# Block 1 of a two-block model: modulation by groups of two chunks, the middle's elementwise work off GpSimd, filling products ahead of the inversion

## The chip, the cores and the metric

One core of one Trainium2 chip runs the whole kernel in one launch. TensorE (PE) multiplies, VectorE (DVE), ScalarE (ACT) and GpSimd (POOL) work elementwise, SyncE (SP) starts most transfers. The metric is the device time of an execution in microseconds (us).

## The reference, cut to what matters

512 tokens of 1024 features pass block 1 and then block 2 (attention, an MLP, a gated recurrence, an MLP). Only block 1 is changed:

```python
mod = jax.nn.silu(c) @ w_ada + b_ada                 # 1024 x 3072 weights, one row c
shift, scale, gate = jnp.split(mod, 3, axis=-1)
p = (x * (1 + scale) + shift) @ w_in                 # 512 x 1024 by 1024 x 3712
# branch A: u = gelu(p_u); v = layer_norm per head(gelu(p_v)) * ln_v_g + ln_v_b;
#           v = causal w_spatial over 128 tokens, per head, + b_spatial; u * v * silu(gate)
# branch B: p + mu * (previous token - p); then a recurrence over the tokens with
#           r, decay w, k, v, a, b for 8 heads of 64; layer norm per head; * silu(gate)
x = layer_norm(ALPHA * x + gate * (concat(A, B) @ w_out))
```

## The kernel before, in words

**Products.** Every operand of a large product is split into a high part (`wh`, `aH`) and the rest (`wl`, `aL`), both of a type that PE takes at full rate, and a product is three matmuls with 512 columns (`mm3`). A weight tile is loaded as `raw`, copied to `wh` by ACT (`copy`, L140) and subtracted to `wl` by DVE or GpSimd (`wsplit`, through `tt`, L123). There are three `raw` buffers and three weight slots.

**Start.** For each of the 8 chunks of 128 features, `load(k)` fetches 512 KB in each of two transfers of `w_ada` (`ada`, its columns for shift and scale), the chunk of `x` (`xt`) and 128 rows of `w_in`; rows of `w_ada` and `x` are 512 bytes long there. `ada_acc` multiplies and adds eight slices on DVE into two accumulators of 128x256 and adds these; two one-column matmuls sum over the partitions; `modulated(k)` turns `x`, applies scale and shift on ACT (`h32`), and makes `hH` (ACT) and `hL` (DVE). The chunk's 18 matmuls into six PSUM tiles follow (four for v of branch A, one each for the decay's and the first k columns). An order token fixes the instruction order of this stage on each engine. Behind it one GpSimd transfer of 2 MB stores ALPHA times x (`xaD`).

**Middle.** The list `ORDER` sets the order of 15 kinds of steps: `r`, `k` (products for branch B with the token shift, `shift_evac`), `A`, `n`, `t`, `m` (loads, layer norm, turns and mixing of branch A), `g` (the elementwise work of a pair of heads for the recurrence), `l` (`lmat`: 64x512 masks out of PSUM into the triangular matrices LB and LK), and `f` (filling products from a queue: V, the gate and u of branch A). `shift_evac` copies a PSUM tile to `sh` (ACT), subtracts neighbours into `shd` (GpSimd) and mixes (DVE, `stt`, L133). PSUM has two buffers `mm` and two `mg`, three `sm` and one `po` in this stage.

**Inversion.** The 32x32 triangular blocks go through DRAM (`scL`) into `XT`, and `inverse()` runs 31 steps of two dependent DVE instructions each (`bz`, then `TV`). On PE `fill(NFILL)` runs filling products meanwhile, three matmuls a step, out of the queue of `ugate` (u and gate of branch A, each a product, a split of weights on GpSimd, and `gt` or `mx` work).

**Chain.** Eight chunks of 64 tokens follow, each merged (`merge`, tiles `Tst`, `M`), with filling products of the four `gate(i)` between them, and `out_gate(k)` sums the third part of `mod` on DVE. Block 2, from about 430 us on, is not touched.

Tiles and order between the tokens come from the framework's scheduler, which fixes each engine's instruction order when the program is built.

## Time and profile before

| | |
|---|---|
| three runs | 1617.93, 1616.04, 1616.99 us (median 1616.99) |
| profiled execution, its own time | 1615.6 us |
| its span in the trace | 1613.8 us |
| PE busy in the span | 1542.8 us, 8293 matmuls |
| DVE, ACT, POOL busy | 939.0, 713.3, 329.5 us |

The stages of block 1 in the trace are the start (0 to 67.3 us, where the first product of the middle begins), the middle (to 179.7, the end of the last triangular mask), a stretch of transfers (to 192.5), the inversion (to 230.3) and the chain (from 239.1, its first merge). In what follows T0 is the first product of the middle. PE is busy for 96% of the span, so it idles for 71 us in all.

### The profile page before, as it was taken

To read this page: it belongs to the slowest core of one execution; us is meant where nothing else is said; L and a number is where in the kernel's file an instruction comes from. 1 tells how busy PE (TensorE), PEld (TensorE's weight loads), DVE (VectorE), ACT (ScalarE), POOL (GpSimd) and SP (SyncE) were. 2 spreads that over 40 slices of the span, in tenths; PEclk is the share of its full clock that TensorE was granted. 3 is DMA by queue.
4 is the path that set the end of the run, shared out by engine and by line. 5 is a ranking of instruction groups with operands and counts; after the bars stand their busy time and mean duration, and the time that the engine had idled before them with its cause. 6 is when DMAs were issued, how large, how long until landed. Compare 5 with 4: busy or idle time off the path is not lost. (4 is left out here: it accounts for less than half of the span.)

```text
span 1613.8 us, 21901 instructions
## 1 busy us (share of the span) xinstructions
PE 1542.8 (96%) x8293; PEld 1305.5 (81%) x8293; DVE 939.0 (58%) x1644; ACT 713.3 (44%) x1297; POOL 329.5 (20%) x459
## 2 busy tenths in 40 slices
PE   5987979999999999999999999999999999999998
PEld 4766768889978899888888887888888988888886
DVE  7797595678667739334343447667754824333445
ACT  3533314655565646333232335667745624322232
POOL 4464732224310023000000033223323200000000
PEclk9998989999999999999999999999999999999999
DMA  9732445544123132333333322322213223231421
GB/s 289 215 97 86 78 130 144 178 132 119 51 70 94 29 105 80 104 103 93 91 93 104 92 91 67 104 79 66 66 53 110 87 79 118 74 110 66 123 86 53
DMA packets 272893, 161.69 MB, mean 100 GB/s; under 512 B 29465, under 2 KB 253316, under 8 KB 272788
## 3 DMA queue, kind: packets, MB, share of 16 engines
q1 hardware_dynamic: 271492, 157.33, 34.2%
q0 software_dynamic: 1152, 2.70, 0.5%
q8 instruction: 65, 1.06, 0.3%
q14 instruction: 40, 0.33, 0.1%
q10 hardware_dynamic: 144, 0.26, 0.0%
HBM read 147.42 MB, written 11.53 MB: 98 GB/s over the span
## 5 line engine op out<-in xcount | busy, mean ns | idle before, releaser
L140 ACT CAST wh<-raw 128x1024 fp32r<-128x1024 f32 (+3 forms) x244 | 242.8, 996 | 466.0 <-PE mm L143 371.2
L123 DVE TENSOR_TENSOR wl<-raw,wh 128x1024 fp32r<-128x1024 f32 (+2 forms) x228 | 272.6, 1197 | 288.1 <-ACT wh L140 284.0
L143 PE MATMUL mm<-bL,wh 128*128 128x512 f32 (+1 forms) x752 | 282.2, 378 | 1.0 <-DVE bL L133 1.0
L143 PE MATMUL mm<-bH,wl 128*128 128x512 f32 (+1 forms) x752 | 281.7, 377 | 0.0
L143 PE MATMUL mm<-bH,wh 128*128 128x512 f32 (+1 forms) x752 | 279.4, 379 | 0.1
L143 PE MATMUL mm<-aH,wh 128*128 128x512 f32 (+1 forms) x656 | 241.0, 369 | 12.3 <-DVE gt L133 9.5
L143 PE MATMUL mm<-aH,wl 128*128 128x512 f32 (+1 forms) x656 | 236.8, 362 | 1.4 <-DVE wl L123 1.4
L143 PE MATMUL mm<-aL,wh 128*128 128x512 f32 (+1 forms) x656 | 237.7, 364 | 0.0
L143 PEld LDWEIGHTS mm<-bL,wh 128*128 128x128 f32 x752 | 141.1, 188 | 29.4 <-DVE bL L133 1.8
L143 PEld LDWEIGHTS mm<-bH,wl 128*128 128x128 f32 x752 | 141.1, 188 | 27.7
L143 PEld LDWEIGHTS mm<-bH,wh 128*128 128x128 f32 x752 | 139.2, 188 | 28.0 <-ACT hg_vt L137 0.5
L143 PEld LDWEIGHTS mm<-aH,wh 128*128 128x128 f32 x656 | 125.2, 191 | 34.4 <-DVE gt L133 10.5
L143 PEld LDWEIGHTS mm<-aH,wl 128*128 128x128 f32 x656 | 125.2, 191 | 20.7 <-DVE wl L123 1.9
L143 PEld LDWEIGHTS mm<-aL,wh 128*128 128x128 f32 x656 | 125.7, 192 | 18.3 <-issue 0.7
L143 PE MATMUL mm<-wh,aH 128*128 128x512 f32 x288 | 113.5, 396 | 1.5 <-ACT aH L140 1.5
L143 PE MATMUL mm<-wh,aL 128*128 128x512 f32 x288 | 112.8, 393 | 0.0
L143 PE MATMUL mm<-wl,aH 128*128 128x512 f32 x288 | 112.6, 393 | 0.0
L140 ACT CAST aH<-t 128x512 fp32r<-128x512 f32 (+1 forms) x74 | 41.1, 564 | 75.7 <-DVE t L123 75.5
L123 POOL TENSOR_TENSOR mlpt<-mlpt,sq 128x256 f32<-128x256 f32 (+1 forms) x9 | 11.9, 1320 | 306.6 <-ACT sq L137 306.6
L245 POOL TENSOR_TENSOR mlpss<-mlpss,pwm 128x1 f32<-128x1 f32 x4 | 2.2, 547 | 322.0 <-DVE mlpss L128 322.0
L123 DVE TENSOR_TENSOR aL<-t,aH 128x512 fp32r<-128x512 f32 (+1 forms) x74 | 45.1, 617 | 36.2 <-ACT aH L140 36.2
L143 PEld LDWEIGHTS mm<-wh,aH 128*128 128x128 f32 x288 | 54.6, 190 | 12.7 <-ACT aH L140 1.9
(545 smaller groups left out, 2819.7 us busy)
## 6 DMA issues: line engine op xcount, KB each, us to landing
raw<-in_mlp_w_dram SPq DMA_DIRECT2D x128, 512.0 KB
raw<-in_hgrn_w_in_dram SPq DMA_DIRECT2D x32, 512.0 KB
raw<-in_w_in_dram SPq DMA_DIRECT2D x23, 512.0 KB
ada<-in_w_ada_dram SPq DMA_DIRECT2D x16, 512.0 KB
raw<-in_w_out_dram SPq DMA_DIRECT2D x10, 512.0 KB
raw<-in_w_ada_dram SPq DMA_DIRECT2D x8, 512.0 KB
raw<-in_mla_w_o_dram SPq DMA_DIRECT2D x8, 512.0 KB
raw<-in_hgrn_w_o_dram SPq DMA_DIRECT2D x8, 512.0 KB
```

The lines of the kernel that those rows point to most:

```text
L123: self.st((eng or self.nc.vector).tensor_tensor(out=out, in0=a, in1=b, op=op))
L140: self.st(self.nc.scalar.copy(out=out, in_=in_))
L143: i = self.nc.tensor.matmul(out, l, r, start=start, stop=stop, **kw)
L245: self.nc.gpsimd.tensor_tensor(out=out, in0=a, in1=cst[: a.shape[0], :n], op=ALU.pow)
```

## The change

Start: loads and modulation go by groups of two chunks. A group is one 512 KB transfer of `x` and four 512 KB transfers of `w_ada`, with rows of 1 KB; one accumulator of 128x512 takes one `ts` and seven `stt`, the first four of them as soon as half of the group is there. The weight split of this stage is on DVE. A chunk's matmuls stand so that those with `hL` come last, and its `x` is turned ahead of the sums. `xaD` is stored by eight SP transfers between loads. The loads of `bsp` and `wsp` (branch A, 0.75 MB) stand among those of the start.

Middle: `shift_evac` is an ACT copy scaled by mu and one `stt` that reads PSUM; the subtraction and the memsets on GpSimd are gone. The row copy of `PC`, the affine `kf` and the broadcast copy `rx` go to ACT; two products and the LK mask go from GpSimd to DVE. The gain of branch A's layer norm is applied in the `stt` that mixes, and its bias comes in over eight small matmuls and four `stt` of 128x128.

Inversion: the first `gate` joins the queue, `NFILL` goes from 61 to 69 steps, and the splits and products of `ugate` go from GpSimd to DVE, at a priority that puts 7 splits, 3 `mx` and 4 `gt` between the steps of the inversion. Chain: `out_gate` uses one accumulator; eight filling steps fewer are left.

```diff
-NFILL = 61
+NFILL = 69
...
-        def ada_acc(acc, raw, steps=range(9)):
+        def ada_acc(acc, raw, steps, q0=0):
 
             for q in steps:
-                if q < 2:
-                    self.ts(acc[q], raw[:, q], sc[:, q : q + 1])
-                elif q < 8:
-                    self.stt(acc[q % 2], raw[:, q], sc[:, q : q + 1], acc[q % 2], ALU.mult, ALU.add)
+                if q == 0:
+                    self.ts(acc, raw[:, q - q0], sc[:, q : q + 1])
                 else:
-                    self.tt(acc[0], acc[0], acc[1], ALU.add)
+                    self.stt(acc, raw[:, q - q0], sc[:, q : q + 1], acc, ALU.mult, ALU.add)
...
-        xa = self.tl(sp, [P, 8, T], "xa", bufs=1)
-
-        def load(k):
+        xa = [self.tl(self.rp, [P, T], f"res{k}") for k in range(8)]
+
+        def load(g):
+
+            xt = self.tl(sp, [P, NB, 2 * P], "xt", bufs=2)
+            gs = slice(2 * g * P, (2 * g + 2) * P)
+            nc.sync.dma_start(out=xt, in_=xv[:, :, gs])
+            ada = []
+            for q in range(2):
+                raw = self.tl(sp, [P, 4, 2, 2 * P], "ada", bufs=4)
+                for j in range(2):
+                    src = w_ada[512 * q : 512 * q + 512, j * D + 2 * g * P : j * D + (2 * g + 2) * P]
+                    nc.sync.dma_start(out=raw[:, :, j, :], in_=src.rearrange("(k p) m -> p k m", p=P))
+                ada.append(raw)
+            return xt, ada, self.tl(sp, [P, 2, 2 * P], "acc")
...
         with self.ordered():
             self.petoken = "start"
-            ada_acc(cur[3], cur[1])
-            w_ = self.wsplit(cur[2], 1, 6 * P, nc.gpsimd)
-            h32 = modulated(0, cur[0], cur[3])
+            pt = turned_x(0, cur[0])
+            part(0, cur, 0)
+            part(0, cur, 1)
+            sums(0, cur)
+            w_ = self.wsplit(rv, 1, 6 * P)
+            modulated(0, pt)
             for k in range(8):
...
                 for tb in range(NB):
-                    s = slice(tb * P, (tb + 1) * P)
-                    self.mm3(psv[tb], hH[k][:, s], hL[k][:, s], wh[:, 0, :T], wl[:, 0, :T], k == 0, k == 7)
+                    self.mm(psv[tb], hH[k][:, tok[tb]], wh[:, 0, :T], k == 0, False)
+                    self.mm(psv[tb], hH[k][:, tok[tb]], wl[:, 0, :T], False, False)
                     if tb == SB and k < 7:
-                        w_ = self.wsplit(cur[2], 1, 6 * P, nc.gpsimd)
-                        h32 = modulated(k + 1, cur[0], cur[3])
...
+                        pt = turned_x(k + 1, (nxt if k % 2 else cur)[0])
+                        if k % 2:
+                            part(g + 1, nxt, 1)
+                            sums(g + 1, nxt)
+                            cur = nxt
+                        w_ = self.wsplit(rv, 1, 6 * P)
+                        modulated(k + 1, pt)
+                        if k % 2 == 0 and k < 6:
+                            part(g + 1, nxt, 0)
...
+                for tb in range(NB):
+                    self.mm(psv[tb], hL[k][:, tok[tb]], wh[:, 0, :T], False, k == 7)
+                for o, pz in oz:
+                    self.mm(pz, wh[:, 0, o : o + P], hL[k], False, k == 7)
             self.petoken = None
-            self.st(nc.gpsimd.dma_start(out=xaD.rearrange("k p t -> p k t"), in_=xa))
+            for k in range(8):
+                nc.sync.dma_start(out=xaD[k], in_=xa[k])
...
-            sh = self.tl(bp, [P, T + 1], "sh", bufs=2)
-            nc.gpsimd.memset(sh[:, 0:1], 0.0)
-            self.copy(sh[:, 1 : T + 1], ps)
-            d = self.tl(bp, [P, T], "shd", bufs=2)
-            self.tt(d, sh[:, 0:T], sh[:, 1 : T + 1], ALU.subtract, nc.gpsimd)
+            sh = shs[0]
+            shs.append(shs.pop(0))
+            self.act(sh[:, 1 : T + 1], ps, AF.Copy, scale=self.pc("mu_b", mc))
             o3 = lambda a: a.rearrange("p (c t) -> p c t", t=RC) if v3 else a
-            self.stt(out, o3(d), self.pc("mu_b", mc), o3(sh[:, 1 : T + 1]), ALU.mult, ALU.add)
+            self.stt(out, o3(ps), omu[:, mc : mc + 1], o3(sh[:, 0:T]), ALU.mult, ALU.add)
...
-            nc.gpsimd.tensor_copy(out=PCt[p], in_=eP[:, :, RC])
+            self.copy(PCt[p], eP[:, :, RC])
...
-            self.ts(kf, t2, hp[:, 8 + p : 9 + p], hp[:, 12 + p : 13 + p])
+            self.act(kf, t2, AF.Identity, scale=hp[:, 8 + p : 9 + p], bias=hp[:, 12 + p : 13 + p])
...
-            self.tt(AR[p][:, :, 1, :], AR[p][:, :, 1, :], eP[:, :, 1 : RC + 1], ALU.mult, nc.gpsimd)
+            self.tt(AR[p][:, :, 1, :], AR[p][:, :, 1, :], eP[:, :, 1 : RC + 1], ALU.mult)
...
-            self.tt(LK[p][hf], LK[p][hf], at(mk2).unsqueeze(1).to_broadcast([P, 4, P]), ALU.mult, nc.gpsimd)
+            self.tt(LK[p][hf], LK[p][hf], at(mk2).unsqueeze(1).to_broadcast([P, 4, P]), ALU.mult)
...
-            v2 = vg.rearrange("p h i -> p (h i)")
-            self.tt(v2, v2, lng, ALU.mult, nc.gpsimd)
-            self.tt(v2, v2, lnb, ALU.add)
-            return v2
+            return vg.rearrange("p h i -> p (h i)")
...
-                    evac(ps)
+                    with tc.high_priority(self.wprio):
+                        evac(ps)
...
-                self.tt(mx, mx, ug, ALU.mult, nc.gpsimd)
+                self.tt(mx, mx, ug, ALU.mult)
...
-                self.stt(t, t, 1.0, ps, ALU.add, ALU.mult)
+                x = self.tl(pool, [P, T], "gbn", bufs=1)
+                self.copy(x, ps)
+                self.stt(t, t, 1.0, x, ALU.add, ALU.mult)
...
-            yield from part_gemm(w_in, j * P, u_evac, nc.gpsimd)
-            yield from part_gemm(w_in, 1024 + j * P, g_evac, nc.gpsimd)
+            yield from part_gemm(w_in, j * P, u_evac)
+            yield from part_gemm(w_in, 1024 + j * P, g_evac)
...
+        queue.append(gate(0, rp))
+        self.wprio = 3000
         fill(NFILL)
+        self.wprio = 400
```

On DVE, in the start, from the accumulation for the second chunk to its modulation, before (`ada` is a slice of `w_ada`, `mod` the modulation):

```order
L128 TENSOR_SCALAR acc_45_208<-ada_200,sc 128x256
L128 TENSOR_SCALAR acc_46_209<-ada_200,sc 128x256
L133 SCALAR_TENSOR_TENSOR acc_45_208<-ada_200,sc,acc_45_208 128x256
L133 SCALAR_TENSOR_TENSOR acc_46_209<-ada_200,sc,acc_46_209 128x256
L133 SCALAR_TENSOR_TENSOR acc_45_208<-ada_200,sc,acc_45_208 128x256
L133 SCALAR_TENSOR_TENSOR acc_46_209<-ada_200,sc,acc_46_209 128x256
L133 SCALAR_TENSOR_TENSOR acc_45_208<-ada_200,sc,acc_45_208 128x256
L123 TENSOR_TENSOR aL_130<-h_41_195,aH_122 128x512
L133 SCALAR_TENSOR_TENSOR acc_46_209<-ada_200,sc,acc_46_209 128x256
L123 TENSOR_TENSOR acc_45_208<-acc_45_208,acc_46_209 128x256
L123 TENSOR_TENSOR mod<-sm_232,bada_111 128x2
```

and now, from the first chunk's split to that of the third:

```order
L122 TENSOR_TENSOR wl_202<-raw_178,wh_201 128x768
L122 TENSOR_TENSOR aL_130<-h_48_205,aH_122 128x512
L122 TENSOR_TENSOR wl_236<-raw_210,wh_235 128x768
L122 TENSOR_TENSOR aL_131<-h_57_239,aH_123 128x512
L127 TENSOR_SCALAR acc_222<-ada_216,sc 128x512
L132 SCALAR_TENSOR_TENSOR acc_222<-ada_216,sc,acc_222 128x512 x3
L132 SCALAR_TENSOR_TENSOR acc_222<-ada_219,sc,acc_222 128x512 x4
L122 TENSOR_TENSOR mod<-sm_282,bada_111 128x2x2
L122 TENSOR_TENSOR wl_289<-raw_262,wh_288 128x768
```

The 128x256 accumulation of every chunk with its closing addition has become one 128x512 accumulation for two chunks, and two weight splits have come in.

On DVE, in the middle, around the first `k` that is not of the start (`vn`, `lw` are branch A's norm, `ld`, `cum`, `kf`, `bz`, `BK` a pair of heads), before:

```order
L123 TENSOR_TENSOR vn_683<-vn_683,lnb 128x512
L590 TENSOR_REDUCE lw_940<-vn_689 128x8
L499 SCALAR_TENSOR_TENSOR cum_804<-m_676,ld_801 128x512
L123 TENSOR_TENSOR kf_814<-kf_814,k_116_661 128x512
L133 SCALAR_TENSOR_TENSOR k_129_759<-shd_794,pb,sh_791 128x512
L123 TENSOR_TENSOR vn_687<-vn_687,lw_928 128x512
L128 TENSOR_SCALAR lw_940<-lw_940 128x8
L123 TENSOR_TENSOR vn_685<-vn_685,lnb 128x512
```

and now:

```order
L122 TENSOR_TENSOR wl_792<-raw_789,wh_791 128x1024
L132 SCALAR_TENSOR_TENSOR AR_93<-po_662,omu,sh_593 128x8x64
L122 TENSOR_TENSOR vn_639<-vn_639,lw_864 128x512
L122 TENSOR_TENSOR wl_877<-raw_874,wh_876 128x1024
L132 SCALAR_TENSOR_TENSOR k_110_701<-mm_708,omu,sh_591 128x512
L129 TENSOR_SCALAR ld_739<-ld_739 128x512
L532 SCALAR_TENSOR_TENSOR cum_742<-m_624,ld_739 128x512
L122 TENSOR_TENSOR kf_752<-kf_752,k_101_613 128x512
```

The mixing `stt` reads the PSUM tile `mm` (or `po`) itself, the bias additions `lnb` have gone, and it stands sooner behind its product.

On DVE, in the inversion's eleventh to thirteenth steps, before:

```order
L123 TENSOR_TENSOR bz_1583<-XT_1581,TV_1582 128x220
L123 TENSOR_TENSOR TV_1582<-TV_1582,bz_1583 128x22x10
L123 TENSOR_TENSOR bz_1583<-XT_1581,TV_1582 128x231
L123 TENSOR_TENSOR TV_1582<-TV_1582,bz_1583 128x21x11
L123 TENSOR_TENSOR bz_1583<-XT_1581,TV_1582 128x240
L123 TENSOR_TENSOR TV_1582<-TV_1582,bz_1583 128x20x12
L133 SCALAR_TENSOR_TENSOR gt_1781<-gt_1781,mm_1756 128x512
L123 TENSOR_TENSOR bz_1583<-XT_1581,TV_1582 128x247
L133 SCALAR_TENSOR_TENSOR gt_1781<-mx_1714,gt_1781 128x512
L123 TENSOR_TENSOR TV_1582<-TV_1582,bz_1583 128x19x13
```

and now:

```order
L122 TENSOR_TENSOR wl_1734<-raw_1731,wh_1733 128x1024
L122 TENSOR_TENSOR tmp_1490<-XT_1488,TV_1489 128x240
L122 TENSOR_TENSOR mx_1621<-mx_1621,gsh_1654 128x512
L122 TENSOR_TENSOR TV_1489<-TV_1489,tmp_1490 128x20x12
L122 TENSOR_TENSOR tmp_1490<-XT_1488,TV_1489 128x247
L122 TENSOR_TENSOR TV_1489<-TV_1489,tmp_1490 128x19x13
L122 TENSOR_TENSOR tmp_1490<-XT_1488,TV_1489 128x252
L122 TENSOR_TENSOR TV_1489<-TV_1489,tmp_1490 128x18x14
L122 TENSOR_TENSOR tmp_1490<-XT_1488,TV_1489 128x255
L122 TENSOR_TENSOR wl_1774<-raw_1771,wh_1773 128x1024
```

Splits (`wl`) and the u products (`mx`) now stand between the dependent pairs.

## Rows read from the trace of the kernel before

**Rows 1.** The page: busy time, share of the span and instructions of each engine.

```profile
PE 1542.8 (96%) x8293; PEld 1305.5 (81%) x8293; DVE 939.0 (58%) x1644; ACT 713.3 (44%) x1297; POOL 329.5 (20%) x459
```

**Rows 2.** Windows: length, busy (x instructions) of PE, PEld, DVE, ACT, POOL; clock; DMA; GB/s.

```profile
16.05:67.30 51.25, 44.94 (x203) 35.17 (x203) 40.47 (x75) 21.40 (x32) 21.61 (x21) 1.00 0.92 254
192.50:239.10 46.60, 35.09 (x143) 27.70 (x142) 44.39 (x93) 8.43 (x11) 15.71 (x10) 0.89 0.44 133
239.10:350.00 110.90, 106.53 (x724) 92.17 (x724) 67.76 (x167) 61.44 (x138) 25.17 (x54) 0.97 0.49 145
...
67.30:179.70 112.40, 97.23 (x530) 79.13 (x530) 90.57 (x121) 46.26 (x70) 64.16 (x71) 0.91 0.36 101
...
4.00:44.00 40.00, 27.13 (x115) 21.45 (x116) 31.46 (x64) 13.92 (x21) 15.28 (x16) 1.00 1.17 314
```

**Rows 3.** Timeline of DVE at the start: start, length, instruction, [idle before <-releaser].

```profile
13.61 0.16 DVE L123 TENSOR_TENSOR mod<-sm,bada 128x2 f32<-128x2 f32 x1 [1.10 <-PE sm L143]
...
20.51 0.16 DVE L123 TENSOR_TENSOR mod<-sm,bada 128x2 f32<-128x2 f32 x1 [1.10 <-PE sm L143]
```

**Rows 4.** Groups of DVE, 4 to 62 us: count, busy, mean ns, idle before.

```profile
L133 DVE SCALAR_TENSOR_TENSOR acc<-ada,sc,acc 128x256 f32<-128x256 f32 x48 | 20.2, 476 | 0.0
L123 DVE TENSOR_TENSOR acc<-acc,acc 128x256 f32<-128x256 f32 x8 | 15.7, 1968 | 0.3
```

**Rows 5.** Waits, 0 to 62 us: in total, times, longest.

```profile
PE sm L143 <- DVE acc L123: 15.6, 7, 9.3
```

**Rows 6.** Timeline of PE: first product of the start, then two products of the middle.

```profile
16.05 0.80 PE L143 MATMUL mm<-wh,aH 128*128 128x512 f32 x1 [1.52 <-ACT aH L140]
...
67.61 0.39 PE L143 MATMUL po<-aL,wh 128*128 128x512 f32 x1
...
71.94 0.39 PE L143 MATMUL po<-aH,wl 128*128 128x512 f32 x1
```

**Rows 7.** Groups of DVE in the middle, 67.3 to 192.5 us.

```profile
L123 DVE TENSOR_TENSOR wl<-raw,wh 128x1024 fp32r<-128x1024 f32 x9 | 14.4, 1602 | 0.9 <-ACT wh L140 0.9
...
L133 DVE SCALAR_TENSOR_TENSOR bz<-AR,pb,kf 128x512 f32<-128x512 f32 x4 | 6.0, 1501 | 0.0
...
L499 DVE TENSOR_TENSOR_SCAN cum<-m,ld 128x512 f32<-128x512 f32 x4 | 4.9, 1213 | 0.0
```

**Rows 8.** Timeline of DVE in the middle.

```profile
91.19 0.74 DVE L133 SCALAR_TENSOR_TENSOR k<-shd,pb,sh 128x512 f32<-128x512 f32 x1
...
93.15 0.74 DVE L133 SCALAR_TENSOR_TENSOR bz<-AR,pb,kf 128x512 f32<-128x512 f32 x1
...
94.42 0.68 DVE L123 TENSOR_TENSOR vn<-vn,lw 128x512 f32<-128x512 f32 x1
...
106.00 1.21 DVE L123 TENSOR_TENSOR wl<-raw,wh 128x1024 fp32r<-128x1024 f32 x1
107.14 1.54 DVE L123 TENSOR_TENSOR vn<-vn,lw 128x512 f32<-128x512 f32 x1
```

**Rows 9.** Groups of POOL in the middle, 67.3 to 192.5 us.

```profile
L123 POOL TENSOR_TENSOR shd<-sh 128x512 f32<-128x512 f32 x13 | 18.9, 1453 | 12.6 <-ACT sh L140 12.5
```

**Rows 10.** Timeline of ACT: the PSUM copy that the `k` of Rows 8 mixes.

```profile
80.20 0.58 ACT L140 COPY sh<-mm 128x512 f32<-128x512 f32 x1
```

**Rows 11.** Waits, 66 to 193 us.

```profile
PE sm L143 <- ACT res L140: 6.7, 2, 6.4
```

**Rows 12.** Timeline of DVE: last mask, inversion's first step, a slowed one, its last.

```profile
179.05 0.68 DVE L123 TENSOR_TENSOR L<-sm,mk 64x512 f32<-64x512 f32 x1 [0.43 <-PE sm L143]
...
192.48 1.01 DVE L123 TENSOR_TENSOR bz<-XT,TV 128x31 f32<-128x31 f32 x1 [7.25 <-DMA raw<-in_w_in_dram]
...
199.57 2.44 DVE L123 TENSOR_TENSOR TV<-TV,bz 128x192 f32<-128x192 f32 x1
...
230.14 0.19 DVE L123 TENSOR_TENSOR TV<-TV,bz 128x31 f32<-128x31 f32 x1
```

**Rows 13.** Timeline of PE: the chain's first merge.

```profile
239.11 1.35 PE L143 MATMUL mg<-Tst,M 128*128 128x64 f32 x8 [2.01 <-DMA Tst<-scT]
```

103 lines of the change are left out of this document (55 added, 48 removed).

## The prediction

> **What bounds the kernel now.** I read the page first, then windows by stage, then timelines, groups and waits of each stage. PE is busy for 1542.8 of 1613.8 us [rows 1], so no change that leaves its matmuls as they are can win more than its 71 idle us and what it does at half clock. The windows [rows 2] place the idle time: about 20 us in the start (6.3 of its last 51.25, and nearly all of the 16.05 before the first product [rows 6]), 15.2 in the middle, 11.5 of the 46.6 around the inversion, 4.4 in the chain's first 111. Each is read by itself.
>
> In the start a chunk takes 6.9 us (from one `mod` to the next, 13.61 to 20.51 [rows 3]). Its 18 products take 18 x 0.228 = 4.1 us at the spacing of 67.61 to 71.94, 19 products apart [rows 6], and four turns bring that to about 4.7. The rest is a round trip: PE waits 15.6 us in 7 times for the accumulator [rows 5], and what closes the accumulator is the addition of 1.97 us, as long as four of the multiply-adds at 0.48 [rows 4], while GpSimd splits weights.
>
> In the middle DVE is busy for 90.6 of 112.4 us and PE for 97.2, the latter at a mean granted clock of 0.91 [rows 2]. The two cross each other: DVE's instructions are stretched (a split takes 1.60 on average, and 1.14 from 106.00 to the next start; `bz` 1.50, and 0.67 at 93.15 [rows 7, 8]), and a product's result passes ACT, GpSimd and DVE before the next step has it: copied at 80.20, mixed at 91.19 [rows 8, 10].
>
> The inversion is DVE's alone: 192.48 to 230.33 [rows 12], and the first merge waits for it until 239.11 [rows 13].
>
> **The change, part by part.** A: the start. DVE's work for two chunks becomes 8 instructions of 128x512 at about 0.66 (0.48 for half the width [rows 4], 0.74 busy for `bz` [rows 8]), two splits at 0.75 x 1.14 = 0.86, two `hL` at 0.6 and small ones: 8.3 us where two periods were 13.8. So DVE and its 2-us addition stop setting the period. Next come PE (9.4 for two chunks) and the loads. A group and two chunks of `w_in` are 2.6 + 0.8 MB, or 10.8 us at the 314 GB/s of 4 to 44 us [rows 2]: the loads are the limit now. Up to the `x` of the last group 14.85 MB must pass, counted from the order of SP's queue (8.4 of `w_ada`, 2.1 of `x`, 2.75 of `w_in`, 0.8 of `bsp` and `wsp`, 0.8 of `xaD` stores, which are new ahead of loads). From 3.2 us, where the first transfers start, that is 50.5 us. Behind it stand turns and sums (1 us), 14 products left of chunk 5 (3.2), chunks 6 and 7 (4.7 and 4.1): T0 is about 64, from 67.3. The first product comes later than before, at about 18, since 2.6 MB and not 1.3 must land for it; the loads cover that. **-3.3**; bounds 0 and -7.8 (18 + 8 x 4.7 + a stall or two, if the loads cost nothing).
>
> The Trainium skill bears on one part of this: DMA: Bandwidth & Descriptors, section Specifications, puts the smallest transfer for line rate at 512 bytes or more, so rows of 1 KB instead of 512 bytes would bring nothing. By it the sum stays as it is. The trace shows 314 GB/s with 512-byte rows and no run yet with the longer.
>
> B: the middle. I counted DVE's instructions up to the last mask in the new order: 13 splits at 1.14, 89 full-width ones at 0.635 (93.15 to 94.42 are two [rows 8]), four scans at 1.2 [rows 7] and some 30 small ones, together about 79 us, where DVE was busy for 90.6. GpSimd's 13 `shd` (18.9 us busy, after waits of 12.6 for the copy [rows 9]) go, and with them the step between ACT and DVE. So PE becomes the limit. Its own time: at a mean clock of 0.91 it spent 2 x 0.09 x 112.4 = 20 us at half clock (1.2 of 2.4 GHz), of which 15.2 can be idle time; at least 5 were work, which full clock does in 2.5. 97.2 - 2.5 is 94.7 us. Some stalls stay: the wait for ACT's copy of a mask (6.4 us once [rows 11]) is untouched, and a PSUM tile is now held until DVE's mixing, about 2.7 us late at its first place. I take 3.3 idle us, T0 + 98 for the last mask instead of T0 + 112.4. The stretch from there to the first inversion step (179.7 to 192.5, stores and loads of `scL` [rows 12]) stays 12.8. **-14.4**; bounds 0 and -20 (DVE's 79 plus masks, PE at a clock it never lost: 92).
>
> C: the inversion. Of its 37.85 us [rows 12] some 3.7 are one V mixing and four `gt`. Eight of its 62 steps are stretched (192.48 the first, 199.57 takes 2.44 where its neighbour of the same width takes 0.35 [rows 12]), by 12.1 together; GpSimd's splits and `mx` run then. 22.0 is left for the steps themselves. Into them come 7 splits at 1.14 and 7 others at 0.6, 12.2: the inversion takes 34.2. GpSimd has nothing left there. PE runs 207 filling matmuls before the first merge and not 183, 207 x 0.228 = 47.2 us, from T0 + 99 to T0 + 146; the merge comes at T0 + 98 + 12.8 + 34.2 + 8.8 = T0 + 153.8 (230.33 to 239.11 is 8.8 [rows 12, 13]), so PE still waits, and DVE's path counts. **-3.7**; bounds -3.7 and +8 (each split also waits for its `wh` from ACT, about 1 us, seven times).
>
> D: the chain. Eight filling steps, 24 matmuls, 5.4 us, are done in time that PE idled before. The chain keeps PE busy for 106.5 of 110.9 us [rows 2], so most of what leaves it shortens it, but filling steps also cover its waits. I take half, **-2.5**; bounds 0 and -5.4. `out_gate`'s two accumulators become one on DVE, which is busy for 67.8 of 110.9 there: nothing, up to 1 us if a merge waits for it.
>
> Sum: -3.3 - 14.4 - 3.7 - 2.5 = -23.9. The profiled execution took 1615.6 us (span 1613.8), so 1591.7; the median of the runs stands 1.4 above that execution: **1593**.
>
> **The rivals.** (1) The loads take all of the start's gain (0 for A): the stores among them wait at the head of SP's queue for ACT, and what is queued behind waits too. The rate of 314 GB/s, which shows no slack, speaks for it. 1596.
>
> (2) Longer rows move faster. T0 then falls to 60, by PE's count: 1589. Beside this: the Trainium skill, SBUF — State Buffer, section The DMA setup-cost knee, advises to coalesce into the largest transfer; `x` alone doubles its size here, so it has little to act on.
>
> (3) The middle's round trips remain at half: `g` still passes ACT, DVE and PE in turn, and two waits of 6 us suffice. B is then -7.2: 1600.
>
> (4) Slower: PSUM tiles are held. Before, ACT's copy at 80.20 freed the tile; now DVE's mixing does, which came 11 us later [rows 8, 10], and with two buffers `mm` the product after the next one must wait for it. A product takes 24 x 0.228 = 5.5 us; what the hold exceeds that costs half of itself for each of 11 products. It takes up the whole gain from a hold of 5.5 + 23.9 x 2 / 11 = 9.8 us, and at the 11 of before it costs 30: 1623. Against it: the new order puts the mixing two or three instructions behind a split instead of behind the whole norm, and DVE's queue is shorter.
>
> **How the numbers follow.** 0.2% (3 us) is about what a measurement of this kernel can tell from no change. My forecast 0.55 (its own range 1585 to 1602: the bounds of C and D and a third of B's), rival 1 0.12, rival 2 0.08, rival 3 0.15, rival 4 0.10. Low end: rival 2 with B some 9 us better, 1580. High end: rival 3 with the 8 of C, 1608. All but rival 4 are faster by over 0.2%, save rival 1 and 3 together with C's bound, where 0.05 falls within 0.2%: faster 0.85, same 0.05, slower 0.10.
>
> **What would show it.** A: `mod` every 10 to 11 us for two chunks, the first product at about 18, T0 at about 64, DMA at over 300 GB/s until 50. B: no `shd`, splits at 1.2 us, the last mask at T0 + 98, PE at a clock near 1.0. C: no step of 2.4 us, the inversion 34 us long, the merge at T0 + 154. D: the chain's stages each a little shorter. It is wrong if PE waits for DVE's `stt` in front of products (rival 4), if the first product slips past 20, or if the inversion passes 40 us.

## The result, and the profile after

The changed kernel is slower: 1626.2 us median of 4 runs (1625.42 to 1628.96), beside 1617.46 for the kernel before on the same chip; the ratio is 1.0054, with a 95% interval of 1.0035 to 1.0074. The forecast was 1593 us, and the range did not hold the time. The profiled execution took 1628.96 us (span 1627.0), against 1615.6 (1613.8) before.

The page of the changed kernel says what was taken away: GpSimd's 329.5 busy us are 240.9, and DVE's 939.0 are 919.3 [rows 1].

```profile
PE 1549.2 (95%) x8309; PEld 1310.4 (81%) x8309; DVE 919.3 (57%) x1617; ACT 720.6 (44%) x1313; POOL 240.9 (15%) x390
```

The windows of the changed kernel, cut at the same places as [rows 2] (start from the first product, middle, inversion to the first merge, chain), with the same columns:

```profile
18.80:78.90 60.10, 49.58 (x198) 40.42 (x199) 34.26 (x52) 23.09 (x34) 2.13 (x9) 0.86 0.73 224
78.90:185.60 106.70, 101.57 (x554) 82.54 (x553) 78.90 (x123) 51.85 (x82) 22.36 (x24) 0.90 0.32 91
197.10:237.60 40.50, 37.69 (x166) 30.57 (x165) 37.35 (x91) 11.15 (x16) 0.95 (x1) 1.00 0.45 134
237.60:353.40 115.80, 101.49 (x704) 87.48 (x704) 71.55 (x169) 60.89 (x138) 18.73 (x32) 0.96 0.48 140
```

The start is 8.9 us longer from its first product, and that comes 2.8 later (18.84 us instead of 16.05). The middle is 5.7 shorter, with DVE busy for the 79 us of the forecast, but PE's clock still at 0.90. The inversion's window is 6.1 shorter, and the chain's 4.9 longer.

To see where the rest of the time goes, I marked the same instructions in each profile: the middle's first product (`po<-aH,wh`), the end of the last mask, the inversion's first and last step, the first merge (`mg<-Tst`), the product that takes `Psb`, the last `su` product of the chain, the first product with a `mla_cH`, the last `lnw` one (the end of block 1) and the last product of `mla_cH` with `wh`, which closes the attention's projections. The span behind that mark is the same within 1.3 us in all kernels. The versions below "after" are the experiments. Columns are start times of PE's instructions, but for the mask and the inversion, which are DVE's (us).

| kernel | middle begins | last mask ends | inversion | first merge | `Psb` product | last `su` | first `mla_cH` | end of block 1 | last `mla_cH` |
|---|---|---|---|---|---|---|---|---|---|
| before | 67.3 | 179.7 | 192.5 to 230.3 | 239.1 | 241.1 | 349.9 | 368.4 | 406.8 | 525.6 |
| after | 78.9 | 185.6 | 197.1 to 229.2 | 237.6 | 246.6 | 353.4 | 376.4 | 416.6 | 538.2 |
| start_alone | 78.5 | 186.4 | 197.9 to 236.9 | 243.7 | 245.9 | 354.6 | 373.5 | 412.0 | 531.2 |
| rest_alone | 71.8 | 173.8 | 184.1 to 218.7 | 229.4 | 231.0 | 337.9 | 359.8 | 405.2 | 524.9 |
| acc_early | 70.8 | 176.9 | 188.8 to 220.9 | 229.4 | 238.8 | 346.2 | 371.1 | 411.7 | 533.6 |
| fill_split | 71.7 | 169.8 | 180.8 to 212.6 | 220.4 | 226.2 | 342.9 | 366.0 | 406.7 | 528.4 |
| after_pad | 79.8 | 185.2 | 193.6 to 226.0 | 235.4 | 245.8 | 352.9 | 376.6 | 416.5 | 537.8 |
| rest_pad | 71.8 | 174.2 | 182.6 to 216.7 | 227.0 | 228.6 | 335.3 | 355.6 | 395.9 | 516.5 |
| before_low | 67.4 | 179.9 | 194.2 to 230.9 | 239.6 | 241.6 | 350.4 | 371.7 | 414.6 | 532.6 |
| acc_early_pad | 62.0 | 164.7 | 173.9 to 208.3 | 218.9 | 221.3 | 328.3 | 350.0 | 389.9 | 512.5 |

The differences of the first two rows, one stage after another, add up: start +11.6, middle -5.7, stores and loads ahead of the inversion -1.3, inversion -5.7, from its end to the `Psb` product +6.6 (17.4 us instead of 10.8), chain -2.0, end of block 1 +6.3 (63.2 us from the last `su` instead of 56.9), attention +2.8: +12.6 of the +13.2. So three stages cost 24.5 us: the start, which the forecast had as a gain, and the way from the inversion to `Psb` and the end of block 1, for which it had no cost.

**The start.** The timeline of DVE in the changed kernel, one group of two chunks:

```profile
31.07 0.16 DVE L122 TENSOR_TENSOR mod<-sm,bada 128x4 f32<-128x4 f32 x1 [1.21 <-PE sm L142]
...
38.80 1.57 DVE L122 TENSOR_TENSOR aL<-h,aH 128x512 fp32r<-128x512 f32 x1 [3.89 <-ACT aH L139]
40.29 0.47 DVE L127 TENSOR_SCALAR acc<-ada,sc 128x512 f32<-128x512 f32 x1
40.80 5.48 DVE L132 SCALAR_TENSOR_TENSOR acc<-ada,sc,acc 128x512 f32<-128x512 f32 x7
48.30 0.16 DVE L122 TENSOR_TENSOR mod<-sm,bada 128x4 f32<-128x4 f32 x1 [2.02 <-PE sm L142]
```

From `mod` to `mod` this group, the second, takes 17.2 us (the ones beside it 13.9 and 16.5), where two chunks took 13.8 [rows 3] and the forecast had 10 to 11. The eight instructions of the accumulation (6 us) are not started when their data land. They stand in DVE's queue behind the odd chunk's `aL`, and that waits 3.9 us for ACT's `aH`, which waits for the odd chunk's turns on PE. Only then does the accumulation run, and PE, which has used up its products, waits for it. The waits of the first 79 us (total, times, longest):

```profile
PE sm L142 <- DVE acc L132: 18.9, 4, 8.4
...
DVE aL L122 <- ACT aH L139: 12.9, 8, 4.1
```

From 40 to 80 us PE's granted clock is 0.83 on average. The accumulation waits for no load here: at 40.29 it starts without idle time ahead of it.

**The first merge.** DVE's timeline:

```profile
240.21 0.94 DVE L132 SCALAR_TENSOR_TENSOR gt<-gt,gbn 128x512 f32<-128x512 f32 x1
244.77 0.69 DVE L122 TENSOR_TENSOR mx<-mx,gsh 128x512 f32<-128x512 f32 x1 [3.62 <-DMA mx<-mixD]
245.49 0.69 DVE L132 SCALAR_TENSOR_TENSOR gt<-mx,gt 128x512 f32<-128x512 f32 x1
246.10 0.41 DVE L122 TENSOR_TENSOR Psb<-mg,ist 128x256 f32<-128x256 f32 x1
```

`Psb`, which the merge needs, stands behind a filling step's `mx`, which waits for its load. The load was late because its issue, at 241.96 in SP's queue, stands behind 16 small transfers, the first merges' `Tst` and `TTb`, from 232.22 on:

```profile
232.22 1.65 SPq L805 DMA_DIRECT2D Tst<-scT  x3
...
241.96 0.33 SPq L689 DMA_DIRECT2D mx<-mixD  x1
```

PE waits 7.9 us for `Psb`.

**The end of block 1.** ACT's timeline of the changed kernel:

```profile
374.28 0.90 ACT L139 CAST aH<-gsh 128x128 fp32r<-128x128 f32 x4 [5.84 <-DVE gsh L122]
...
375.71 2.16 ACT L139 CAST mla_cH<-raw 128x512 fp32r<-128x512 f32 x4
```

The casts of the last weights of `w_out` (`mla_cH`) stand behind the last post's casts (`aH<-gsh`), for which ACT idles 5.84 us. Before, all six stood ahead of them:

```profile
363.06 1.14 ACT L140 CAST mla_cH<-raw 128x512 fp32r<-128x512 f32 x2 [1.76 <-DMA raw<-in_w_out_dram]
...
371.62 0.90 ACT L140 CAST aH<-gsh 128x128 fp32r<-128x128 f32 x4 [0.78 <-DVE gsh L123]
```

Nothing in the diff touches these lines. PE waits 3.0 us for `res` and 2.3 for `mla_cH`, in a stretch where it waited 0.7 before.

### The profile page after: what moved, and what is told of

Its sections match the earlier page's. It is cut to its first block, busy times and chain, and to the rows that moved or that the text cites. A ratio compares the mean times of both kernels' runs of the same rounds, so it can differ in the third digit from the quotient of the medians.

```text
span 1627.0 us, 21813 instructions
## 1 busy us (share of the span) xinstructions
PE 1549.2 (95%) x8309; PEld 1310.4 (81%) x8309; DVE 919.3 (57%) x1617; ACT 720.6 (44%) x1313; POOL 240.9 (15%) x390
## 5 line engine op out<-in xcount | busy, mean ns | idle before, releaser
L122 DVE TENSOR_TENSOR wl<-raw,wh 128x1024 fp32r<-128x1024 f32 (+3 forms) x244 | 286.3, 1175 | 310.4 <-ACT wh L139 306.0
L142 PE MATMUL mm<-aH,wh 128*128 128x512 f32 (+1 forms) x656 | 239.6, 367 | 5.8 <-DVE res L132 3.0
L142 PE MATMUL mm<-wh,aL 128*128 128x512 f32 x288 | 108.9, 394 | 0.0
L142 PEld LDWEIGHTS mm<-wh,aH 128*128 128x128 f32 x288 | 55.2, 192 | 13.1 <-ACT aH L139 1.8
L122 DVE TENSOR_TENSOR aL<-t,aH 128x512 fp32r<-128x512 f32 (+1 forms) x74 | 45.0, 617 | 36.5 <-ACT aH L139 36.5
L142 PEld LDWEIGHTS mm<-wh,aL 128*128 128x128 f32 x288 | 55.2, 192 | 12.0
L142 PEld LDWEIGHTS mm<-wl,aH 128*128 128x128 f32 x288 | 55.3, 192 | 11.1
```

The costliest lines, as they stand in the source:

```text
L122: self.st((eng or self.nc.vector).tensor_tensor(out=out, in0=a, in1=b, op=op))
L142: i = self.nc.tensor.matmul(out, l, r, start=start, stop=stop, **kw)
```

## The experiments

Fourteen kernels ran, for four theories. The expectations use the letters A and B anew in each run, so two of them go by name here: the queue theory, that the start's accumulation is late by its place in DVE's queue, and the `mx` theory, that `mx` ahead of `Psb` costs the merge. The clock theory (C in the expectations) is that idle time of PE costs the middle its clock; the shared-memory theory (E), on the end of block 1, came last. Times stand beside runs of the kernel before on the same chip (1617.1, 1617.7, 1616.9, 1616.8).

**start_alone, rest_alone.** Each half of the change alone: the start with the one-accumulator `out_gate` in the kernel before, and everything else with the start of before.

> The kernel before with the new start alone (loads and modulation by groups of two chunks), together with the one accumulator of the output gate; middle, inversion and chain as before. Theory A (the start itself loses 7.3 us): the first product of the middle at 74 to 75 us, the time 1622 to 1626. Rival (the start is late in the changed kernel only because of what else it loads there, bsp and wsp): at 67 to 70, 1616 to 1619.

> The changed kernel with the start of the kernel before (loads and modulation chunk by chunk); middle, inversion and chain as changed. Account from the profiled executions: against the kernel before the rest gains 5.8 us in the middle (counted from its first product), 1.3 in the transfers, 5.7 in the inversion and 2 in the chain, and loses 6.5 at the first merge and some 10 at the end of block 1 and in the attention behind it. Theory A (the start is most of the loss, the rest about breaks even): first product of the middle at 67 us, the time 1616 to 1621. Rival (the rest gains once the start does not delay it): below 1612.

start_alone: 1622.14 us, ratio 1.0031 [1.0020, 1.0043]; the middle begins at 78.5, as in the changed kernel, and both are as the expectation's theory A had them: the start loses this by itself, without `bsp` and `wsp` among its loads. rest_alone: 1617.23, ratio 1.0001 [0.9990, 1.0013], in the range of its theory A too. It is 12.0 us ahead of before at the last `su` and has 0.7 left at the last `mla_cH`: from the middle's first product to the last `su` the new middle, inversion and chain earn 16.5 us of the 20.6 that the forecast had for them, and the end of block 1 takes most of it back. Its middle begins late, at 71.8 and not 67: PE waits 5.8 us for DVE's `tw`, which reads the PSUM bank that the middle's first tile `po` is given, and `tw` itself stood 2.75 us for the store of `xaD`. That is a hold of the kind of rival 4, at another place.

**acc_early.** Both halves of the next group's accumulation ahead of the odd chunk's `modulated`, in a place where their data are there:

```diff
                         if k % 2:
-                            part(g + 1, nxt, 1)
                             sums(g + 1, nxt)
                             cur = nxt
                         w_ = self.wsplit(rv, 1, 6 * P)
-                        modulated(k + 1, pt)
                         if k % 2 == 0 and k < 6:
                             part(g + 1, nxt, 0)
+                            part(g + 1, nxt, 1)
+                        modulated(k + 1, pt)
```

> The changed kernel, with the accumulation for the next group placed on DVE ahead of the low part of the odd chunk instead of behind it; nothing else moves. Theory A (the start is late because the 6 us of accumulation begin only when DVE's wait for that chunk's ACT copy is over): the period of 16.9 us for two chunks falls to 11 to 12, the first product of the middle comes at 63 to 67 us instead of 74.6, and the time falls by 7 to 11 us, to 1615 to 1619. Theory B (the loads set the start, with the stores of xaD that stand among them in SP's queue): the first product of the middle stays above 72 and the time above 1624.

1619.49 us, ratio 1.0016 [1.0002, 1.0029]. The middle begins at 70.8 instead of 78.9: the queue theory held, though not to the 64 us of the forecast. The expectation's mark, the first product of the last chunk, is at 66.4, inside its 63 to 67; the time fell by 6.7 us, a little less than the 7 to 11 expected. ACT waited 20.1 us for rows of `w_in`, 9.7 in the changed kernel, and DVE behind it 5.6 in one go.

**mx_two, both.** Two buffers for `mx`, so that its load need not wait for the buffer (`tmp` of the inversion halved to make room); and this together with acc_early.

```diff
-            mx = self.tl(pool, [P, T], "mx", bufs=1)
+            mx = self.tl(pool, [P, T], "mx", bufs=2)
```

> The changed kernel with a second buffer for the tile mx of the u gate, so that its load needs not wait for the product before (the scratch tile of the inversion is cut to the half that it uses, to make room). Theory A (the load of the fourth mx stands in SP's queue behind the 16 small loads of the first merges, DVE waits for it and the copy that the first merge needs is queued behind it): PE's wait of 7.9 us in the first merge falls below 1.5 and the time by 5 to 8 us, to 1618 to 1621. Theory B (PE would wait there for something else, or the chain gives the time back): 1624 to 1627.

> The two edits of the other runs together (accumulation ahead of the odd chunk's low part, two buffers mx). Theory A: the gains add up, 12 to 18 us, to 1608 to 1614, faster than the kernel before. Theory B: at most 3 us below the changed kernel.

mx_two: 1628.44, ratio 1.0067 [1.0046, 1.0089], no gain, where 5 to 8 us were expected. DVE's timeline at the first merge shows that the cure failed:

```profile
241.50 0.69 DVE L132 SCALAR_TENSOR_TENSOR gt<-mx,gt 128x512 f32<-128x512 f32 x1
247.45 0.29 DVE L127 TENSOR_SCALAR ga<-raw,sc 128x128 f32<-128x128 f32 x1 [5.25 <-DMA raw<-in_w_ada_dram]
247.65 0.42 DVE L122 TENSOR_TENSOR Psb<-mg,ist 128x256 f32<-128x256 f32 x1
```

`mx` is in time, and now `ga` waits, 5.25 us, for the next load behind the same `Tst` and `TTb`. So `mx` was not the cause: the `mx` theory fell, and the expectation's rival (its theory B), that PE would wait there for something else, held. Any load behind the merges' transfers is late, and whatever in-order queue has its consumer ahead of the merge's work stops. both: 1621.58, ratio 1.0019 [1.0005, 1.0034], no better than acc_early, and 4.6 us below the changed kernel where 12 to 18 were expected.

**psb_first.** `both`, with the first merge's `Psb` ordered by hand ahead of these waiters, and the filling work between the first merges behind `start(2)`:

```diff
+            if c == 0:
+                self.token = "inverse"
             self.tt(Psb, q4(ps[:, : 4 * RC]), ist.unsqueeze(1).to_broadcast([P, 4, RC]), ALU.add)
+            self.token = None
...
-        with first():
-            for _ in between(0, ()):
-                pass
         start(2)
+        with first():
+            for _ in between(0, ()):
+                pass
```

> The version with both edits (early accumulation, two buffers mx) and one instruction moved: the copy Psb of the first merge stands on DVE ahead of the third accumulation of the output gate, whose load it waited for there (5.3 us of waiting in the run with both edits). Theory A: PE's wait for Psb falls from 10.2 us to below 3 and the time by 5 to 8 us, to 1613 to 1617. Rival (the chain's own round trips set its end, so the head start is lost in it): Psb comes early, the last chunk's end moves by less than 3 us and the time stays above 1619.

1622.78, ratio 1.0033 [1.0019, 1.0048]; 1613 to 1617 were expected, and the rival there, above 1619, held. The `Psb` product comes 13.6 us behind the inversion's end instead of 17.4 to 19.1, but the chain is 117.1 long, from 107 to 108. PE's wait for `Psb` is 4.7 us, where it was to be below 3, and PE's waits name the next queue, ACT's, where a cast of a late weight stands ahead of the merge's `Bt` and `Kt`. (In `both` the cast already stood there, without a wait.)

```profile
PE ss L142 <- ACT Kt L139: 6.3, 3, 5.7
PE mg L142 <- DVE Psb L122: 4.7, 1, 4.7
```

**fill_as_before.** The filling work ahead of the inversion as it was (`NFILL` 61, no gate and no priority of 3000).

> The changed kernel without its third part: no gate in the queue, 61 filling steps and not 69 ahead of the first merge, and the results of the filling products at the ordinary priority; start and middle as changed. Theory A (the copy Psb of the first merge is late because DVE's order now has u's product and the next load's accumulation ahead of it, which wait for loads): PE's wait for Psb falls from 7.9 us to below 2; the chain then has 8 steps more to do, so that the time falls by 2 to 6 us, to 1620 to 1624. Rival (the wait comes from the splits on DVE, which stay): the wait stays above 6, the time within 2 us of the changed kernel or above.

1628.76, ratio 1.0073 [1.0054, 1.0092]. The `Psb` product comes 11.3 us behind the inversion's end, nearly as before (10.8): the eight steps, the gate and their priority brought the wait. But the inversion takes 35.0 us, and the end of block 1 is 65.3: nothing is won, where 2 to 6 us were expected.

**fill_split.** psb_first with two of seven filling steps moved behind the next mask:

```diff
-ORDER = "r0 A0 k1 g0 k2 r1 g0 n0 r2 f11 g0 f1 t0 g1 m0 g1 k3 g1 g2 l0 g2 r3 g3 l1 g2 f7 l2 g3 l3 f2 l4 g3 l5 f5 l6 l7"
+ORDER = "r0 A0 k1 g0 k2 r1 g0 n0 r2 f11 g0 f1 t0 g1 m0 g1 k3 g1 g2 l0 g2 r3 g3 l1 g2 f5 l2 g3 f2 l3 f2 l4 g3 l5 f5 l6 l7"
```

> As psb_first, with two of the seven filling steps in the middle moved between two masks, where PE idled 1.6 us for an ACT copy and then ran at half clock for 15 us. Theory C (that idle time costs the clock): the idle time goes, the granted clock stays near 1.0 there, and the last mask comes 4 to 8 us sooner after the middle's first product (106 us in the changed kernel, to 98 to 102). Rival (the small products of the masks themselves, which follow one another there, cost the clock): the clock falls as before, the last mask within 2 us of psb_first.

1620.37, ratio 1.0015 [1.0003, 1.0026]. Windows of the middle, of the changed kernel and of fill_split:

```profile
160.00:180.00 20.00, 18.92 (x72) 15.55 (x73) 12.56 (x20) 7.01 (x11) 6.38 (x10) 0.57 0.25 58
```

```profile
71.70:169.80 98.10, 91.93 (x550) 74.84 (x549) 78.30 (x123) 51.79 (x82) 21.92 (x24) 0.99 0.35 99
```

In the changed kernel PE is busy for 18.9 of these 20 us at a mean clock of 0.57, so for most of them at the lower of the two levels (1.2 of 2.4 GHz). What stands ahead is one gap, for ACT's copy of a mask:

```profile
161.08 1.99 PE L142 MATMUL sm<-AR,BK 64*128 64x128 f32 x8 [1.57 <-ACT res L139]
```

With the other order the clock is 0.99, and the middle takes 98.1 us, the forecast's number. In psb_first, the same but for these two steps, it takes 102.2 at 0.95. So the order is worth 4.1 us here; the other 4.5 from the changed kernel's 106.7 came in psb_first already, and what brought them I did not find.

That the idle time is what costs the clock, as the clock theory has it, is not shown. fill_split idles at the same place, and longer; psb_first has the changed kernel's gap:

```profile
152.10 1.16 PE L142 MATMUL sm<-AR,BK 64*128 64x128 f32 x8 [1.80 <-ACT res L139]
```

```profile
152.86 2.07 PE L142 MATMUL sm<-AR,BK 64*128 64x128 f32 x8 [1.57 <-ACT res L139]
```

Behind the gap fill_split keeps the full clock (1.00 from 149 to 165 us), and psb_first is at the lower level for some 7 us and not 17. What else differs is what PE did just before: in the changed kernel and in psb_first only products of 64x128 and 128x2, in fill_split six products of 512 columns among them.

**after_pad, rest_pad, rest_split_pad.** The end of block 1 remained. The addresses in the built programs tell what changed there. The pool of the shifted rows has four tiles of 2 KB before (`sh` and `shd`, two each) and three after, so all that lies behind it moves by 1.9 KB: `gw`, the 128 bytes of the post's statistics, from 161568 to 163488. `mla_cH0` is put at 162656 to 164704 when the chain's pool closes. So in the changed kernel its first write must wait until the last post has used `gw`, and with it come the five other casts in ACT's order, and the last loads of `w_out`, which wait for the buffers that these casts free. A fourth buffer undoes that:

```diff
-        shs = [b([P, T + 1], f"sh{i}") for i in range(3)]
+        shs = [b([P, T + 1], f"sh{i}") for i in range(4)]
...
-        tmp = self.tl(rp, [P, T], "tmp", bufs=1)
+        tmp = self.tl(rp, [P, T // 2], "tmp", bufs=1)
```

> The changed kernel with a fourth buffer among the shifted-row tiles (2 KB more in the pool below the chain's pool; the inversion's scratch tile is halved to make room). By it the chain's tiles lie 2 KB lower, where they lay in the kernel before, and the one small statistics tile of the last post (gw) no longer shares memory with the first of the six tiles mla_cH. Theory E (the loss at the end of block 1 comes from that shared memory: mla_cH cannot be written until the last post has read gw, its casts stand behind the last post's casts in ACT's order, the last load of w_out waits for their buffer): from the last su to the last mla product 176 to 179 us instead of 184.8, as before and start_alone have (175.7, 176.6), the order on ACT again mla_cH ahead of the last aH<-gsh, time 1616 to 1620. Rival (the end of block 1 is late for another reason, the order only shows it): from the last su to the last mla product 183 us or more, time above 1623.

> The kernel before's start with the changed middle, inversion and chain (rest_alone, 1617.2), with the same fourth buffer. Theory E: the 12 us that rest_alone was ahead at the last su are kept to the end: from the last su to the last mla product 176 to 179 us instead of 187, time 1607 to 1611, faster than before by 0.4 to 0.6%. Rival: as rest_alone, 1615 to 1619.

> rest_pad with the order of the filling products of fill_split alone (two of the seven steps ahead of the second mask moved behind it; without the other edits of that run). Theory C (the middle's rest is TensorE at half clock after a wait, and products between the masks prevent it): granted clock of the middle 0.97 or more instead of 0.94, last mask 2 to 4 us earlier than in rest_pad, time 1604 to 1608. Rival (the earlier middle only waits longer at the first merge, whose loads stand behind others in SP's queue): the first merge's wait grows by what the middle gains, time as rest_pad within 2 us.

rest_pad: 1606.33, ratio 0.9938 [0.9921, 0.9955], 10.9 us below rest_alone and a little below the 1607 to 1611 expected; the casts stand ahead again, and the end of block 1 takes 60.6 us instead of 67.3. after_pad: 1625.49, ratio 1.0052 [1.0034, 1.0069]: no gain that can be measured (1616 to 1620 were expected), and 63.6 us at the end of block 1, from 63.2, with the order mended: the rival of that expectation came out. Here the fifth load of `w_out` is 2.4 us late for ACT and PE waits 3.2 for `res` behind it, with or without the order. rest_split_pad: 1608.7, ratio 0.9945 [0.9931, 0.9958]: the middle is 99.0 us at a clock of 0.97 (102.4 at 0.94 in rest_pad, so the order keeps the clock a second time), the inversion ends 4.6 earlier, and the `Psb` product comes 0.9 later: PE waits 7.0 for `Psb`. The time is 2.4 us above rest_pad's, and the rival there held in kind: the loads set the first merge, and an earlier inversion only waits.

**before_low, acc_early_pad, fill_as_before_pad.** The kernel before with 1 KB that nothing uses ahead of `mla_cH0`, which lays it over the last 64 bytes of `gw`, and two earlier experiments with the fourth buffer.

```diff
         self.mla_rope = x_("COS"), x_("SIN")
+        self.mla_x.tile([P, 256], F32, tag="low", name="mla_low")
```

> The kernel before with a tile of 1 KB that nothing uses in the pool of mla_cH, so that mla_cH0 lies 1 KB lower and shares memory with the last post's statistics tile gw, as in the changed kernel; no work is added or taken away. Theory E (that shared memory sends the casts of mla_cH behind the last post's in ACT's order): until the last su as before (349.9), from there to the last mla product 182 to 187 us instead of 175.7, time 1623 to 1628. Rival (the order at the end of block 1 comes from the new middle's timing, the memory is incidental): order and time as before, 1615 to 1619.

> acc_early (1619.5, both halves of a group's accumulation ahead of the odd chunk's subtraction) with the fourth buffer of after_pad. If the late start covers what the buffer gives: with the start 8 us earlier the gain shows, last su to last mla product 181 or less (acc_early 187.4), time 1610 to 1614. If the first merge's wait covers it (it is in this kernel too): time 1617 to 1620, as after_pad beside the changed kernel.

> fill_as_before (1628.8, the filling work ahead of the inversion as in the kernel before, no wait at the first merge) with the fourth buffer of after_pad. If the first merge's wait covers what the buffer gives: last su to last mla product 178 to 181 instead of 185.6, time 1619 to 1623. If the late start covers it: time 1626 to 1629.

before_low: 1624.02, ratio 1.0041 [1.0028, 1.0054]. No work was added, all is as before to the last `su` (350.4), and the end of block 1 takes 64.2 us instead of 56.9. ACT's timeline has the changed kernel's order:

```profile
370.45 0.69 ACT L140 CAST aH<-gsh 128x128 fp32r<-128x128 f32 x3
371.05 2.17 ACT L140 CAST mla_cH<-raw 128x512 fp32r<-128x512 f32 x4
377.80 1.14 ACT L140 CAST mla_cH<-raw 128x512 fp32r<-128x512 f32 x2 [4.57 <-DMA raw<-in_w_out_dram]
```

So the shared-memory theory is shown by itself: 7 us for 64 shared bytes, and PE waits 2.7, 1.3 and 0.8 us there. fill_as_before_pad: 1615.77, ratio 0.9990 [0.9981, 0.9999], 13.0 below fill_as_before and below the 1619 to 1623 expected. acc_early_pad: 1603.36, ratio 0.9920 [0.9907, 0.9934], 16.1 below acc_early and the fastest of all; the expectation had 1610 to 1614 by a gain behind the last `su` (to the last `mla_cH` 181 us or less). That stretch is 184.2, from 187.4, so most of the gain lies ahead of it: the middle begins at 62.0, from 70.8. SP's queue of acc_early shows what stands among the start's loads there:

```profile
17.26 1.90 SPq L365 DMA_DIRECT2D ada<-in_w_ada_dram  x2
19.21 3.46 SPq L601 DMA_DIRECT2D bsp<-in_b_spatial_dram  x3
22.99 0.92 SPq L365 DMA_DIRECT2D ada<-in_w_ada_dram  x2
23.96 3.27 SPq L601 DMA_DIRECT2D bsp<-in_b_spatial_dram  x3
27.33 1.48 SPq L374 DMA_DIRECT2D raw<-in_w_in_dram  x3
...
30.30 1.11 SPq L601 DMA_DIRECT2D bsp<-in_b_spatial_dram  x2
```

Eight small `bsp` loads hold SP for 7.8 us. With the fourth buffer the scheduler puts them behind the start (from 79 us in after_pad, 62.45 in acc_early_pad). The 0.5 MB of `wsp` went with them, and no run moves the `bsp` loads alone: that their time in SP's queue is the cause is argued from the queue. In the changed kernel they cost nothing by themselves, since the accumulation is later still: start_alone, which has them behind the start, begins its middle at 78.5. DVE's timeline of acc_early_pad then has the period that the forecast had for the start, 10.96 us:

```profile
28.03 0.16 DVE L122 TENSOR_TENSOR mod<-sm,bada 128x4 f32<-128x4 f32 x1 [0.61 <-PE sm L142]
...
38.99 0.16 DVE L122 TENSOR_TENSOR mod<-sm,bada 128x4 f32<-128x4 f32 x1 [0.61 <-PE sm L142]
```

The windows of acc_early_pad, cut as those of the changed kernel above, start and middle:

```profile
18.80:62.00 43.20, 41.76 (x199) 34.35 (x200) 33.12 (x52) 23.11 (x34) 1.04 (x8) 1.00 0.84 284
62.00:164.70 102.70, 95.05 (x551) 77.11 (x550) 79.27 (x123) 51.95 (x82) 24.66 (x25) 0.96 0.37 102
```

## Why the prediction was wrong

It said faster, and the time is slower. One of its steps failed (A), one was mis-sized (B), two held in kind (C and D), and two losses were in no step. The forecast was -23.9 and the marks show +12.6. The 36.5 us between them are A 14.9, B 8.7, the first merge 6.6, the end of block 1 6.3, the attention 2.8 and D 0.5, less 1.3 for the transfers ahead of the inversion and 2.0 for C.

**A, the start: failed (-3.3 forecast, +11.6 measured).** The working added up what DVE does in a group, 8.3 us, and took the loads as the limit. It did not ask what stands ahead of the accumulation in DVE's queue. In the code one half is written behind the odd chunk's `modulated` and the other ahead of the next group's sums, so both stand behind the odd chunk's `aL`, which waits for ACT and PE; the new order that stands with the change has all eight instructions there. So the group's work on DVE, ACT and PE runs in turn and not side by side, and a period is 14 to 17 us. acc_early moves only these lines and takes back 8.1 us, acc_early_pad 16.9: with the place mended and SP's queue without `bsp` and `wsp`, the middle begins at 62.0, 2 us earlier than the forecast's 64. The sum was right for another order than the one in the diff. Of the rivals of the start none was this: rival 1 named SP's queue and not DVE's.

**B, the middle: right in its mechanism, mis-sized (-14.4 forecast, -5.7 measured).** DVE's load (78.9 us for 79) and the end of `shd` came as said. The term that failed is "3.3 idle us" beside PE at full clock: at a clock of 0.90, PE was busy for 101.6 us and not for 94.7, which is 6.9 of the 8.7 us, and idle for 5.1. Rival 3 (waits remain, -7.2) is nearest in size, but its two waits of 6 us are not there (the longest is 1.6), so that is luck. With another order of the same products fill_split takes the forecast's 98 us and is busy for 91.9 (550 matmuls; 554 in the changed kernel), so the size was one of the clock and not of the work. What the chip's clock went by stays open: 17 us at the lower level follow an idle 1.57 us, but behind the same gap psb_first has some 7, and fill_split none behind 1.80.

Rival 4 (1623, slower) is near the measured time, but what it rests on is seen only for 1.5 us in the changed kernel's middle, a wait for DVE's `k` at 98.24. The time was slower for other reasons.

**C, the inversion: held in kind (-3.7 forecast, -5.7 measured, outside the bounds of -3.7 and +8).** It takes 32.2 us from the first step to the last. There is no step of 2.4 us: the first, 1.01 long before [rows 12], is now (its scratch tile has a new name)

```profile
197.07 0.19 DVE L122 TENSOR_TENSOR tmp<-XT,TV 128x31 f32<-128x31 f32 x1 [6.71 <-DMA raw<-in_w_in_dram]
```

and the 192-wide one, 2.44 before, is

```profile
201.77 0.36 DVE L122 TENSOR_TENSOR TV<-TV,tmp 128x192 f32<-128x192 f32 x1
```

The splits and products between them cost what was put down each, but only 5 splits, 3 `mx` and 4 `gt` stand between the steps, and not 7, 3 and 4: 9.9 us by the forecast's prices instead of 12.2, which is the 2 us beyond the forecast. The steps without stretch agree with the Trainium skill, SBUF — State Buffer, section Who interferes with whom: an instruction of DVE with two inputs in SBUF contends with one of GpSimd that reads SBUF. GpSimd has 0.95 busy us left there.

**The first merge: a step that was missing (+6.6).** The forecast took the 8.8 us from the inversion to the merge over, and let the filling work do no harm there. More filling steps and a gate mean more loads just behind the merges' transfers in SP's queue, and more consumers of them ahead of the merge in DVE's and ACT's. mx_two and psb_first show that mending one consumer gives the wait to the next; fill_as_before, that the added work is its cause. In acc_early_pad the same filling work costs 2.2 us (13.0 from the inversion's end to the `Psb` product, 10.8 before): SP issues the load of `mx` at 208.09 there, ahead of the merges' transfers from 213.41 on. What put it ahead, I did not settle.

**D, the chain: nearly as forecast (-2.5 forecast, -2.0 measured).** 704 matmuls instead of 724 stand in it; PE's busy time fell by 4.7 us and its idle time grew by 2.7, so about half of what left was won, as the forecast took it.

**The end of block 1: a step that was missing (+6.3), and nothing in the diff's lines tells it.** A temporary pool that became 2 KB smaller moved the tiles behind it, and a tile of the next stage came to lie on 128 bytes that are used last. before_low shows the size of it alone (+7.2 us in the medians and +7.3 at the end of block 1), rest_pad, fill_as_before_pad and acc_early_pad its undoing: 11 to 16 us, of which the end of block 1 accounts for 4 to 8. The rest of these gains comes ahead of it, in acc_early_pad from the start (by SP's queue, as argued above), in fill_as_before_pad from an inversion that begins 6.4 us earlier, which I did not trace further. In the changed kernel itself the shared bytes are not shown to be what sets the +6.3: after_pad mends the order of the casts and is as late there (63.6 us from the last `su`, from 63.2), with the fifth load of `w_out` 2.4 us late for ACT with or without the order.

**What stays open.** The attention is 1 to 4 us longer in each version with the new middle than before (from the end of block 1 to the last `mla_cH` 122.6 us in acc_early_pad, 118.8 before; before_low 118.0). Its instructions stand in a slightly different order; I made no experiment on it. And after_pad: that its late start and its wait at the merge cover the fourth buffer's gain agrees with the two runs in which one of them was taken away, but that the late load explains the 63.6 us at its own end of block 1 is argued, and why that load is later than in rest_pad is not shown.

Against the forecast's sum, acc_early_pad stands so: start -5.3 (forecast -3.3), middle -9.7 (-14.4), to the inversion -3.6 (0), inversion -3.4 (-3.7), from it to the `Psb` product +2.2 (0), chain -1.8 (-2.5), behind it +8.5 (0): -13.1 of -23.9.

## What to carry to other kernels

An engine's work per period says nothing until one has read what stands ahead of it in its in-order queue: an accumulation whose data are there is worth its place ahead of every instruction that waits for another engine, and small loads in a load queue may count by their issue time (here 7.8 us for eight, which is argued from the queue). When a late stage changes though no line of it did, compare where its tiles lie: a pool that became smaller elsewhere can lay a tile on one that is read last, and a spare buffer of 2 KB can be worth more than the change: in rest_pad it gave 10.9 us, to a change that had brought nothing. A gain ahead of a load-bound point is not a gain; look first at whether what follows could start earlier.

## What the runs showed of the hardware

The start's loads moved faster with rows of 1 KB than with rows of 512 bytes. In the start the kernel before moved 314 GB/s [rows 2] (from 4 to 30 us too), the changed one 334 from 4 to 30 us, with `bsp` between its loads, start_alone 357 and acc_early_pad 376, both without `bsp` there (the window of acc_early_pad from 4 to 30 us):

```profile
4.00:30.00 26.00, 14.23 (x59) 11.75 (x60) 16.43 (x25) 7.81 (x12) 9.04 (x26) 1.00 1.08 376
```

The DMA engines are full in both (a share of 1.17 before and 1.08 here). So rival 2's higher rate was there, with 62 GB/s. The Trainium skill, DMA: Bandwidth & Descriptors, section Specifications, puts the smallest transfer for line rate at 512 bytes or more, by which longer rows would bring nothing; the rates here differ, but the transfers of `x` became larger too, and how much of it is the row's length alone was not measured.

TensorE stayed at the lower of its two levels (1.2 of 2.4 GHz) while it was busy. In the changed kernel, behind a single gap of 1.57 us and through products of 64x128 and full-width ones:

```profile
161.00:178.00 17.00, 16.92 (x64) 14.11 (x65) 10.40 (x17) 4.99 (x10) 4.38 (x5) 0.51 0.23 51
```

Behind a gap of the same length psb_first is there for some 7 us (0.57 from 152 to 160 us, 1.00 from 160 to 172), and fill_split behind 1.80 us not at all, but behind its next gap, of 1.28 us, for some 3. So the length of the gap does not tell how long the lower level lasts, and no run here shows what does.
